# A row-sum kernel's last block: four loads of rows and two of columns regrouped into three and two

## The chip, the cores and the metric

The kernel runs on one core of one Trainium2 chip. The metric is the device time of that core in microseconds (us).

Two lengths appear. The *time* is what the timed runs give (163.94 us before). The *span* is what the profile covers of one execution (162.3 us).

## The reference

```python
def reference(x, multiplier):          # x: 32 x 512 x 1024 float32, multiplier 0.5
    return (np.sum(x, axis=-1) * multiplier).astype(np.float32)
```

There are 16,384 rows of 1024 numbers, 67.1 MB in all. Each row becomes one number.

## The kernel before

Each of the 128 partitions owns 128 consecutive rows. They are loaded in 8 blocks of 16 rows (8 MB each) into three rotating buffers. The first seven blocks are each one load. VectorE sums eight rows with one reduction, and ScalarE sums the other eight, one instruction a row, with the accumulator output.

The last block is loaded in pieces that get smaller, so that little work is left when the last bytes arrive. A row on VectorE is here a "half-add": one instruction adds the two halves of the row element by element and accumulates the total.

```python
    def dve_span(t, r, lo, hi, dst, start=0.0):      # VectorE, line 57
        mid = (lo + hi) // 2
        nc.vector.tensor_tensor_reduce(
            out=t[:, r, lo:mid], in0=t[:, r, lo:mid], in1=t[:, r, mid:hi],
            scale=mul, scalar=start, op0=ADD, op1=ADD, accum_out=dst)

    # ... seven blocks: one load, reduce_sum of 8 rows (line 73), act_row of 8 rows (line 47) ...

    c0 = (n_blocks - 1) * B
    t = x_pool.tile([P, B, D], fp32, name="xb")
    cut = 768
    pieces = [(0, 8), (8, 12), (12, 14), (14, 15)]
    for lo, hi in pieces:
        nc.sync.dma_start(out=t[:, lo:hi, :], in_=x_rows[:, c0 + lo : c0 + hi, :])
    for lo, hi in ((0, cut), (cut, D)):
        nc.sync.dma_start(out=t[:, B - 1, lo:hi], in_=x_rows[:, c0 + B - 1, lo:hi])
    on_act = {4, 5, 6, 7, 10, 11, 13}
    for r in range(B - 1):
        if r in on_act:
            act_row(t, r, c0 + r)
        else:
            dve_span(t, r, 0, D, res[:, c0 + r : c0 + r + 1])
    dve_span(t, B - 1, 0, cut, part)                                  # "first span"
    dve_span(t, B - 1, cut, D, res[:, rows - 1 : rows], start=part)   # "second span"

    nc.sync.dma_start(out=out_view, in_=res)                          # the store
```

## Time and profile before

| | before |
|---|---|
| time, median of 3 runs | 163.94 us (163.76 to 164.02) |
| span of the profiled execution | 162.3 us |
| share of the span: VectorE, ScalarE | 42%, 42% |
| read from memory | 67.11 MB, 414 GB/s over the span |

DVE is VectorE, ACT is ScalarE, SPq is the sync engine, which issues the transfers (DMA), and L57 is line 57 of the kernel. These are lines of the profile's page: the span, the engines' busy shares, what keeps each engine busy in 40 equal slices (a digit is the busy share in tenths), and the chain of waits that ended last, by line.

```profile
span 162.3 us, 234 instructions
DVE 68.2 (42%) x34; ACT 67.9 (42%) x127; POOL 0.2 (0%) x4
...
DVE  0000039800596007940099101990049700697452
ACT  3000039700595007930099101990039600696870
...
DMA  7979979979979979979989998998998997998990
...
DMA xb<-in_x_dram 85%; DVE sums L73 11%; SPq L90 1%; DVE xb L57 0%; SPq L71 0%; DVE part L57 0%; DVEq L135 0%
```

The DMA row is nearly full throughout (the packets took 96.5% of the span of the 16 DMA engines), while both compute engines pause in every block. The chain is 85% load. The 11% on VectorE are two reductions that release a buffer, after which the next load is queued long before its turn (the one issued at 51.09 landed 49.58 us later). So the kernel is a stream of loads, and everything ahead of the last block's own loads is out of reach of a change to that block.

The end of that chain, in order of time (start, length, what):

```profile
111.36 47.37 DMA xb<-in_x_dram
158.73 0.02 issue
158.75 0.35 DVE xb L57
159.11 0.13 issue
159.24 0.09 DVE part L57
159.33 0.03 issue
159.36 0.35 DVE xb L57
```

The timeline of the same end shows each instruction (start, length, engine, line, operation; in brackets the idle time before it and what ended it):

```profile
157.80 0.69 DVE L57 CUSTOM_DVE_ANT_0 xb<-xb 128x512 f32<-128x512 f32 x1 [0.58 <-DMA xb<-in_x_dram]
...
158.75 0.56 DVE L57 CUSTOM_DVE_ANT_0 xb<-xb 128x384 f32<-128x384 f32 x1 [0.26 <-DMA xb<-in_x_dram]
...
159.36 0.35 DVE L57 CUSTOM_DVE_ANT_0 xb<-xb,part 128x128 f32<-128x128 f32 x1
...
159.78 0.35 SPq L104 DMA_DIRECT2D out_dram<-res  x1
```

The first span starts when its 768 columns land, at 158.73. The second span has no bracket: its own 256 columns landed at 159.06, while VectorE was still on the first span. So the end hangs on the landing of the *first* part, then two half-adds in a row, then the store. Between the last landing (159.06) and the end of the span lie 3.2 us, 2% of the span. That is all the tail there is to save.

### The profile page before, as it was taken

What the parts mean: (1) busy time and instruction counts of PE and PEld (TensorE: products, weight loads), DVE (VectorE), ACT (ScalarE), POOL (GpSimd) and SP (SyncE); (2) the same over time, 40 slices, a digit from 0 to 9 for tenths busy, and PEclk for the clock granted to TensorE, in tenths of its full rate; (3) what the DMA queues carried; (4) which work ended last, traced back from release to release, by engine and by line L of the source; (5) the groups of instructions that cost most, each with busy time, mean ns of one, the idle gap of its engine ahead of it and who ended that gap; (6) DMA issues with size and microseconds to landing.
All of it is one profiled execution on the core that took longest, in us unless ns stands there. A gap on an engine that the chain in (4) does not pass through costs nothing.

```text
span 162.3 us, 234 instructions
## 1 busy us (share of the span) xinstructions
DVE 68.2 (42%) x34; ACT 67.9 (42%) x127; POOL 0.2 (0%) x4
## 2 busy tenths in 40 slices
DVE  0000039800596007940099101990049700697452
ACT  3000039700595007930099101990039600696870
POOL 0000000000000000000000000000000000000000
DMA  7979979979979979979989998998998997998990
GB/s 258 517 307 469 517 323 452 517 323 452 517 323 452 517 323 452 517 323 452 517 372 406 517 404 372 517 404 372 517 404 372 517 436 339 436 444 384 416 383 21
DMA packets 2017, 67.18 MB, mean 414 GB/s; under 512 B 224, under 2 KB 480, under 8 KB 736
## 3 DMA queue, kind: packets, MB, share of 16 engines
q1 hardware_dynamic: 2016, 67.18, 96.5%
q14 instruction: 1, 0.01, 0.0%
HBM read 67.11 MB, written 0.07 MB: 414 GB/s over the span
## 4 chain that ended last, share of the span: by engine, by line
DMA 85%; DVE 11%; SPq 1%; issue 0%; DVEq 0%
DMA xb<-in_x_dram 85%; DVE sums L73 11%; SPq L90 1%; DVE xb L57 0%; SPq L71 0%; DVE part L57 0%; DVEq L135 0%
## 5 line engine op out<-in xcount | busy, mean ns | idle before, releaser
L47 ACT ACTIVATE xb<-xb 128x1024 f32<-128x1024 f32 x63 | 65.6, 1042 | 89.1 <-DMA xb<-in_x_dram 89.1
L73 DVE TENSOR_REDUCE sums<-xb 128x8 f32<-128x8192 f32 x7 | 60.8, 8686 | 86.1 <-DMA xb<-in_x_dram 86.1
L47 ACT ACTIVATION_READ_ACCUMULATOR xb<-xb 128x1 f32 x63 | 11.7, 186 | 0.0
L57 DVE CUSTOM_DVE_ANT_0 xb<-xb 128x512 f32<-128x512 f32 (+1 forms) x9 | 5.8, 674 | 5.2 <-DMA xb<-in_x_dram 5.2
L47 ACT ACT_TABLE_LOAD x1 | 1.3, 1283 | 0.7 <-PEq L121 0.7
L76 DVE TENSOR_SCALAR res<-sums 128x8 f32<-128x8 f32 x7 | 1.2, 172 | 0.2
L57 DVE DVE_READ_ACCUMULATOR2_ANT res<- 128x1 f32 x9 | 0.7, 81 | 0.0
L57 DVE CUSTOM_DVE_ANT_0 xb<-xb,part 128x128 f32<-128x128 f32 x1 | 0.3, 350 | 0.0
L121 POOL MEMSET const-bfloat16-1.0<- 128x1 bf16 x1 | 0.1, 102 | 0.0
L121 POOL MEMSET const-uint8-127<- 128x1 uint8 x1 | 0.1, 102 | 0.0
L121 POOL MEMSET const-float32-1.0<- 128x1 f32 x1 | 0.1, 99 | 0.0
L121 POOL MEMSET const-float32-0.0<- 128x1 f32 x1 | 0.1, 98 | 0.2 <-issue 0.2
L57 DVE DVE_READ_ACCUMULATOR2_ANT part<- 128x1 f32 x1 | 0.1, 83 | 0.0
## 6 DMA issues: line engine op xcount, KB each, us to landing
xb<-in_x_dram SPq DMA_DIRECT2D x1, 4096.0 KB, 39.7
xb<-in_x_dram SPq DMA_DIRECT2D x1, 2048.0 KB, 44.2
xb<-in_x_dram SPq DMA_DIRECT2D x1, 1024.0 KB, 46.2
xb<-in_x_dram SPq DMA_DIRECT2D x1, 512.0 KB, 46.9
xb<-in_x_dram SPq DMA_DIRECT2D x1, 384.0 KB, 47.4
xb<-in_x_dram SPq DMA_DIRECT2D x1, 128.0 KB, 47.2
xb<-in_x_dram SPq DMA_DIRECT2D x7, 49.5
out_dram<-res SPq DMA_DIRECT2D x1, 64.0 KB, 1.5
```

What stands on the lines that cost most here:

```text
L47: nc.scalar.activation(out=t[:, r, :], in_=t[:, r, :], func=mybir.ActivationFunctionType.Copy, scale=mul, accum_out=res[:, col : col + 1],)
L57: nc.vector.tensor_tensor_reduce(out=t[:, r, lo:mid], in0=t[:, r, lo:mid], in1=t[:, r, mid:hi], scale=mul, scalar=start, op0=ADD, op1=ADD, ...
L73: nc.vector.reduce_sum(out=sums[:, c0 : c0 + h], in_=t[:, 0:h, :], axis=mybir.AxisListType.X)
L76: nc.vector.tensor_single_scalar(out=res[:, c0 : c0 + h], in_=sums[:, c0 : c0 + h], scalar=mul, op=mybir.AluOpType.mult,)
L90: nc.sync.dma_start(out=t[:, lo:hi, :], in_=x_rows[:, c0 + lo : c0 + hi, :])
L121: nc = _bacc.Bacc("TRN2", target_bir_lowering=False, num_devices=1)
```

## The change

The intent is to have one load fewer in the last block, and to give the last row's two parts sizes such that the second part lands about when VectorE is done with the first.

```diff
-    cut = 768
-    pieces = [(0, 8), (8, 12), (12, 14), (14, 15)]
+    cut = 640
+    pieces = [(0, 8), (8, 13), (13, 15)]
...
-    on_act = {4, 5, 6, 7, 10, 11, 13}
+    on_act = {4, 5, 6, 7, 11, 12, 14}
```

## The prediction

> **What bounds the kernel now.** It is a stream of loads. The chain of waits is 85% load and 11% one VectorE reduction (which only paces when a buffer comes free). 67.1 MB are read at 414 GB/s over the 162.3 us span; VectorE and ScalarE are each busy only 42%. The load engines show 97 to 99% busy up to the last block. Only the tail can react to this diff: the last block's loads are issued at 109.4 us, long before their turn, and everything before is untouched.
>
> **The tail now** (timeline, and the moments at which each load's completions arrive). The first 8 rows land at 149.11, then 4 rows at 154.00 (4.89 us), 2 rows at 156.49 (2.49), 1 row at 157.77 (1.28), 768 columns at 158.73 (0.96), 256 columns at 159.06 (0.33). VectorE starts the 768-column half-add at 158.75 (559 ns), reads its accumulator, and starts the 256-column one at 159.36 (350 ns), which therefore no longer waits for its own load: it waited for the previous span. It ends at 159.71; the store is issued at 159.78, and lands at 161.33. So the end is set by landing of the 768 columns + 0.61 + 0.35 us, then the store. [...]here the store took 1.55 us, and the change doesn't touch it.
>
> **What the change does.** The bytes are the same; one load fewer.
> 1. Loads. In the tail packets took 1213, 611, 309, 159, 124 and 46 ns for 32, 16, 8, 4, 3 and 1 KiB: about 0.038 ns/B plus about 8 ns. Each DMA engine moves 8 packets of a load, so one load fewer saves about 8 x 8 ns plus one 9 ns completion packet, 0.07 us. [...]Estimated landings: 8 rows 149.11, 5 rows 155.2, 2 rows 157.70, 640 columns 158.51, 384 columns 158.99.
> 2. Rows. Row pace is 0.615 us on VectorE and 1.04 us on ScalarE. Rows 8 to 10 and 11, 12 are done by 157.1 and 157.4, before the next load. Row 13 (VectorE) runs 157.72 to 158.4, free before the 640 columns land; row 14 (ScalarE) ends with its accumulator read at about 158.87. Neither is last.
> 3. The end. 640 columns: half-add about 0.49 us (559 minus 64 elements at 1 ns), so the second span starts at 158.53 + 0.54 = 159.07, just after its own load (158.99). It takes about 0.415 us (350 plus 64 elements), ending at 159.49 instead of 159.71. Store and end follow 0.22 us sooner.
>
> All of the gain, about 0.2 us, lies on the critical path, but it's 0.13% of the time; runs of before alone spread by 0.26 us. The whole stretch after the last landing is 3.2 us, 2% of the span, so a gain above 2% is not available, and a loss of 3.3 us would need a failure of the stream.
>
> **Predicted:** 163.73 us, range 163.40 to 164.00.
>
> **What would show it.** Right: last landing about 0.07 us sooner; the last two half-adds about 0.49 and 0.41 us, the second ending 0.2 us sooner; ScalarE's last row ending before it. Wrong: ScalarE's row 14 ends last, the larger 5-row load lands late enough to delay rows 11, 12 past 157.7, or 2560- and 1536-byte packets cost more than the line above says.
>
> **What would make it wrong.** Run-to-run drift larger than the effect; another rate on the next chip; the load start or a buffer's release shifting by chance.

## The result, and the profile after

| | before | after |
|---|---|---|
| time, median of 6 runs each | 163.97 us (163.76 to 164.09) | 163.84 us (163.62 to 164.17) |
| ratio, 95% interval | | 0.9994 (0.9981 to 1.0008) |
| span of the profiled execution | 162.3 us | 161.9 us |

A ratio here is the mean time of one kernel's runs over the mean of the other's in the same rounds, so it is not quite the ratio of the medians. The difference is far below 2%, and the interval includes 1.

The chain and the timeline of the changed kernel end so:

```profile
110.52 47.69 DMA xb<-in_x_dram
158.21 0.02 issue
158.23 0.49 DVE xb L57
158.72 0.02 DVE part L57
158.74 0.08 issue
158.82 0.42 DVE xb L57
```

```profile
157.41 1.06 ACT L47 ACTIVATE xb<-xb 128x1024 f32<-128x1024 f32 x1 [0.30 <-DMA xb<-in_x_dram]
...
158.23 0.49 DVE L57 CUSTOM_DVE_ANT_0 xb<-xb 128x320 f32<-128x320 f32 x1
158.37 0.19 ACT L47 ACTIVATION_READ_ACCUMULATOR xb<-xb 128x1 f32 x1
...
158.82 0.42 DVE L57 CUSTOM_DVE_ANT_0 xb<-xb,part 128x192 f32<-128x192 f32 x1
...
159.32 0.35 SPq L104 DMA_DIRECT2D out_dram<-res  x1
```

The two half-adds took 0.49 and 0.42 us, and ScalarE's last row ended at 158.56 (158.37 + 0.19), 0.26 us before the second of them started, all as predicted. The store is issued at 159.32 instead of 159.78.

Is that 0.46 us of gain? No. The right way to read a change in the tail of a stream is from a common point close ahead of it. The last full block is the same work in both kernels, and it landed at 139.40 us in one execution and at 139.08 us in the other. This splits the difference of the two profiled executions:

| stretch | before | after | difference |
|---|---|---|---|
| start of span to landing of last full block | 139.40 | 139.08 | -0.32 |
| that landing to issue of the store | 20.383 | 20.237 | -0.146 |
| issue of the store to its landing | 1.546 | 1.550 | 0.00 |
| landing of the store to end of span | 0.939 | 1.001 | +0.062 |

The first row is code that the change didn't touch. The last row was expected by nobody. These two rows, and whether 0.146 us can be believed at all, are what the experiments are about. "L" below stands for the landing of the last full block, and all stretches are counted from it.

### The profile page after: what moved, and what is told of

It reads as the page before. It is cut to its first block, busy times and chain, and to the rows that moved or that the text cites. A ratio compares the mean times of both kernels' runs of the same rounds, so it can differ in the third digit from the quotient of the medians.

```text
span 161.9 us, 233 instructions
## 1 busy us (share of the span) xinstructions
DVE 68.1 (42%) x34; ACT 67.9 (42%) x127; POOL 0.2 (0%) x4
## 4 chain that ended last, share of the span: by engine, by line
DMA 85%; DVE 11%; SPq 1%; issue 0%; DVEq 0%
DMA xb<-in_x_dram 85%; DVE sums L73 11%; SPq L90 1%; DVE xb L57 1%; SPq L71 0%; DVE part L57 0%; DVEq L135 0%
```

## The experiments

All twelve runs are here, in the order of their questions. The times of the kernel before beside them are from the same chip and the same rounds.

### What a measurement here can resolve

Edit: none, in two runs: the kernel before as it is, and the changed kernel as it is.

> The kernel before, unchanged, measured as if it were a change: the noise floor. Both theories: ratio 1.000 with an interval of about 0.1% to each side, so about 0.2 us, as wide as the effect that the change should have. In the profile, from the landing of the last full block to the issue of the store: 20.38 us within 0.03 us (20.383 in the first profile). If that stretch repeats so closely, it can measure the change where the total time cannot; if it moves by 0.1 us or more between executions of the same kernel, the 0.15 us seen in the first pair of profiles proves nothing.

> The changed kernel once more. Theory (the tail is shorter by 0.15 us, the rest of the difference between the first two profiles is drift of the stream): last full block to store issue 20.24 us within 0.03, total 0.1 to 0.2 us below the kernel before. Rival (the change also speeds the whole stream, which was 0.32 us ahead by the last full block in the first pair of profiles): last full block again lands 0.3 us sooner than in the profiles of before, and the total is 0.4 us lower.

Measured:

| run | median, us | before, us | ratio, 95% interval | L | L to store | landing to end |
|---|---|---|---|---|---|---|
| placebo | 163.89 | 163.91 | 0.9999 (0.9983 to 1.0016) | 139.19 | 20.387 | 0.939 |
| after_again | 163.76 | 163.91 | 0.9987 (0.9970 to 1.0003) | 139.28 | 20.215 | 1.001 |

The stretch from L to the store repeats to 0.004 us for the kernel before (20.383 and 20.387) and to 0.022 us for the changed one (20.237 and 20.215). So the 0.16 us between their means is real, although no interval of the total time could show it: those are about 0.3% (0.5 us) wide from end to end. L itself went from 139.08 to 139.28 for the changed kernel and from 139.40 to 139.19 for the kernel before, so the 0.32 us of the first pair was drift of the stream, and the rival that credited it to the change falls. The 0.062 us at the end of the span repeats exactly.

### Which half of the change gives what

```diff
 # cut_only: the kernel before, with
-    cut = 768
+    cut = 640
 # rows_only: the changed kernel, with
-    cut = 640
+    cut = 768
```

> The six loads and row shares of before, with only the cut of the last row moved from 768 to 640. Theory: landings after the last full block at 9.71, 14.61, 17.10, 18.38, 19.20, 19.68 us; second span starts at 19.81, store issue at 20.31 us, so 0.07 us of the 0.15. Rival (all the gain is one load fewer): 20.38, as before. Total time: same within noise under both.

> The new row pieces and row shares, with the old cut of 768. Theory: 9.71, 15.81, 18.31, 19.27, 19.60 us after the last full block, second span at 19.90, store issue at 20.32 us: 0.06 us of the 0.15 from one load fewer. Rival (the gain is all in the cut): 20.38. Total time: same within noise under both.

Measured:

| run | loads in last block | L to store | landing to end | L to end of span | ratio, 95% interval |
|---|---|---|---|---|---|
| before, placebo | 6 | 20.383, 20.387 | 0.939 | 22.868, 22.870 | |
| cut_only | 6 | 20.273 | 0.940 | 22.757 | 0.9996 (0.9981 to 1.0011) |
| rows_only | 5 | 20.315 | 1.001 | 22.869 | 1.0000 (0.9986 to 1.0015) |
| after, after_again | 5 | 20.237, 20.215 | 1.001 | 22.788, 22.771 | |

Both halves bring the store forward: the cut by 0.11 us (0.07 was expected; its last columns landed at 19.65 and not at 19.68), the load saved by 0.07 us, together about the 0.16 us of the whole change. But the 0.062 us at the end of the span comes with the load saved, and returns almost all of its 0.07 us. Counted to the end of the span, regrouping the rows gained nothing (22.869 against 22.868 and 22.870); the moved cut alone did all of it, and the full change is not better than cut_only.

### What a queued load costs, and how far merging may go

```diff
 # many_loads: the changed kernel, with
-    pieces = [(0, 8), (8, 13), (13, 15)]
+    pieces = [(r, r + 1) for r in range(B - 1)]
 # seven_rows: the changed kernel, with
-    pieces = [(0, 8), (8, 13), (13, 15)]
+    pieces = [(0, 8), (8, 15)]
```

> The changed kernel, but its first 15 rows of the last block in 15 loads of one row instead of 3: 12 loads more, each of 8 packets per DMA engine. Theory (a queued load costs only its packets' overhead, 8 x 8 ns plus a 9 ns completion): last landing and store issue 0.9 us later, store issue at 21.15 us after the last full block, total +0.9 us against the changed kernel. Rival 1 (bytes alone count): no change. Rival 2 (each load carries a fixed cost like the store's 1.5 us from issue to landing): +18 us.

> One step further in the direction of the change: rows 8 to 14 in one load of seven. Theory (merging rows is free only while the merged rows are computed before the last columns land): the seven rows land at 18.22 us after the last full block; VectorE then has 4 rows at 0.615 us before the last row's spans, so store issue at 21.76 us, 1.5 us later than in the changed kernel, although the last columns land 0.07 us sooner; total +1.5 us. Rival (fewer loads are always better in this stream): total 0.07 us lower.

Measured:

| run | median, us | before, us | ratio, 95% interval | L to last columns | L to store | landing to end |
|---|---|---|---|---|---|---|
| after_again (its times, from another chip, are above) | | | | 19.58 | 20.215 | 1.001 |
| many_loads | 164.56 | 164.08 | 1.0029 (1.0012 to 1.0046) | 20.45 | 21.074 | 0.853 |
| seven_rows | 165.53 | 164.08 | 1.0083 (1.0064 to 1.0103) | 19.50 | 21.728 | 1.059 |

With 12 more loads the store came 0.85 us later than in the changed kernel (21.074 less 20.226, the mean of its two profiles): 0.071 us a load. Neither rival fits. The end of the span shrank again, to 0.853 us, so that from L to the end it is 0.60 us more than before (23.471 against 22.869); the medians of the total differ by 0.48 us, the same within their noise. Against the changed kernel +0.9 us was expected in the total; the two were not timed in the same rounds, and from L to the end the difference is 0.69 us, because the end shrank.

In seven_rows the last columns land 0.08 us *sooner*, and the store comes 1.5 us *later*. Its timeline shows why (start, length, engine, operation):

```profile
157.71 0.69 DVE L57 CUSTOM_DVE_ANT_0 xb<-xb 128x512 f32<-128x512 f32 x1 [5.85 <-DMA xb<-in_x_dram]
...
159.55 0.69 DVE L57 CUSTOM_DVE_ANT_0 xb<-xb 128x512 f32<-128x512 f32 x1
...
160.16 0.49 DVE L57 CUSTOM_DVE_ANT_0 xb<-xb 128x320 f32<-128x320 f32 x1
...
160.69 0.42 DVE L57 CUSTOM_DVE_ANT_0 xb<-xb,part 128x192 f32<-128x192 f32 x1
```

VectorE idles 5.85 us for the seven rows, then has four of them back to back, and the last row's spans have to queue behind (no bracket at 160.16), although their columns had landed at 158.96. Merging rows was free here only as long as the merged rows were computed before the last columns arrived. The change's groups of five and two rows stay within that limit; one step further costs 1.5 us in the store's issue, against 0.16 us that the whole change gains there.

### Where the cut should be, and a wait that costs more than it should

```diff
 # cut512 and cut896: the changed kernel, with
-    cut = 640
+    cut = 512     # or 896
```

> The changed kernel with cut 512. Both theories: columns land at 18.97 and 19.61 us after the last full block, and the second span now truly waits for its own load. Theory (a wait for a load ends 0.02 us after it lands, as at the other loads): second span starts at 19.63, takes 0.48, store issue at 20.19 us, 0.05 sooner than the changed kernel. Rival (this instruction, which waits for its load and for the first span's sum, takes about 0.13 us from the later of the two, as the changed kernel's trace showed: landing 158.683, sum read by 158.73, start 158.817): start 19.75, store issue 20.31 us.

> The changed kernel with cut 896, away from the balance point on the other side. Theory: the first part lands at 19.43 us after the last full block, its half-add takes 0.62 us, second span starts at 20.12 and takes 0.28, store issue at 20.48 us: 0.24 us later than the changed kernel, though the last columns land at the same time. Rival (only the last landing sets the end): 20.24 or sooner, since the last span is shorter.

Measured from L, in us:

| run | first part lands | second part lands | second span starts | it takes | store |
|---|---|---|---|---|---|
| cut896 | 19.39 | 19.57 | 20.08 | 0.28 | 20.450 |
| after | 19.12 | 19.60 | 19.74 | 0.42 | 20.237 |
| cut512 | 18.98 | 19.59 | 19.73 | 0.48 | 20.297 |

Their total times tell nothing: cut896 164.20 us, ratio 1.0005 (0.9989 to 1.0022), and cut512 163.97 us, ratio 0.9996 (0.9977 to 1.0015), with 164.08 us for the kernel before.

Cut896 is as the theory said: a late and long first span pushes the second one, wherever the last landing is. For cut512 the theory falls and the rival holds. The second span now has the load as the last thing it waits for, and yet starts 0.13 us after the landing. In the records of all fourteen profiles, an instruction of VectorE or ScalarE whose only wait is for its load starts 0.02 to 0.03 us after the landing if it was idle until then. The chain of cut512 has two pieces there that such landings lack: a queue instruction (DVEq) and 0.09 us of "issue".

```profile
158.90 0.03 issue
158.92 0.02 DVEq L57
158.94 0.09 issue
159.03 0.48 DVE xb L57
```

The second span has two things to wait for: its load, and the first span's sum (`part`). The trace's own records show a separate semaphore instruction ahead of it on VectorE, which waits for the load (158.923 to 158.944); the half-add itself carries the wait for `part`. A semaphore is in these records a counter: in the kernel before, the landing of the last columns raises semaphore 105 until 159.060, and the separate instruction, from 159.088 to 159.109, waits for 105.

The same pattern stands in the kernel before, on the first half-add of the last block. It also has two waits: for its 8 rows, which landed at 149.106, and for ScalarE, which had been done for 40 us. The next piece's half-add waits for its load alone, which landed at 154.002:

```profile
149.25 0.69 DVE L57 CUSTOM_DVE_ANT_0 xb<-xb 128x512 f32<-128x512 f32 x1 [0.94 <-DMA xb<-in_x_dram]
...
154.03 0.69 DVE L57 CUSTOM_DVE_ANT_0 xb<-xb 128x512 f32<-128x512 f32 x1 [2.24 <-DMA xb<-in_x_dram]
```

The first starts 0.145 us after its landing, the second 0.024 us. The next run takes the second wait away by giving a wrong result in each partition's last row:

```diff
 # cut512_nosum: cut512, with
-    dve_span(t, B - 1, cut, D, res[:, rows - 1 : rows], start=part)
+    dve_span(t, B - 1, cut, D, res[:, rows - 1 : rows])
```

> The kernel of cut512, but its second span no longer takes the first span's sum as its start, so it waits for its load alone; the last row of each partition is wrong on purpose. Theory (an instruction with two waits gets the first one as an instruction of its own ahead of it, and the two together take 0.13 us after the landing): without the second wait the span starts 0.02 to 0.03 us after the landing at 19.59, so at 19.62 instead of 19.73 us after the last full block, and the store issue comes at 20.19 instead of 20.30. Rival (the delay belongs to the short last load or to an engine that was idle): still 19.73.

Measured: wrong as intended, one time of 163.80 us, state unknown, so only its profile counts. The columns land at 19.58 us after L, the second span starts at 19.61, the store is issued at 20.113.

```profile
158.94 0.02 issue
158.96 0.42 DVE xb L57
```

The wait is back to 0.02 us, so the theory of this run holds: the second wait is what costs the extra 0.11 us. The edit takes away two things at once, though, the wait and the start that is read from memory. That the start is not the cause is shown by the first half-add of the last block: its start is a constant, and it takes 0.144 us from landing to start even in this run, where it still has its two waits (0.138 to 0.145 us in the thirteen profiles in which the landing is its last wait). And a part nobody had predicted: the same half-add of 256 elements took 0.42 us instead of 0.48. Its start is now a constant and no longer a number for each partition read from memory.

### The end of the program

The runs so far had shown different times from the store's landing to the end of the span, and always the same for the same number of loads. The records of the sync engine explain it. When the program ends, that engine waits for the kernel's semaphores one after another in a fixed order. Here are the start times of these steps, relative to the store's landing, in us (the views of the profile leave semaphore instructions out; these are from the trace's records):

| step waits for semaphore | before (store signals 106) | after (store signals 105) | tiny3, below (store signals 108) |
|---|---|---|---|
| 104 | -1.146 | -1.150 | -1.144 |
| 105 and 103 | -1.088 | **0.016** | -1.085 |
| 106 and 100 | **0.016** | 0.078 | -1.024 |
| 107 and 99 | 0.081 | 0.142 | -0.960 |
| 108 and 102 | 0.142 | 0.204 | **0.016** |
| 101, then the closing barrier | 0.207 | 0.269 | 0.081 |
| end of span | 0.939 | 1.001 | 0.813 |

Steps ahead of the store's semaphore are done during the 1.1 us in which the store is under way. Those behind it come after, at 0.06 us each. The transfers take eight semaphores in turn (99, 100 and 103 to 108 in the records), so one load fewer moved the store from 106 to 105, one step earlier. Two earlier runs agree: the store of many_loads signalled 99, which the table has between 106 and 108 (0.853 us to the end, between 0.939 and 0.813), that of seven_rows 104, in the first step (1.059 us). If that is the cause, any extra transfer repairs it, even one that brings nothing:

```diff
 # tiny1 and tiny3: the changed kernel, with, in the loop over blocks after the load
+        if b == 2:
+            for k in range(1):        # tiny3: range(3)
+                scrap = res_pool.tile([P, 1], fp32, name=f"scrap{k}")
+                nc.sync.dma_start(out=scrap[0:1, :], in_=x_rows[0:1, 0, k : k + 1])
```

> The changed kernel plus one load of 4 bytes, issued while the queue waits for a buffer, its result unused. Theory (at the end of the program the sync engine waits for the kernel's load semaphores one after another in a fixed order, 0.06 us a step, and only the steps behind the store's own semaphore come after its landing; one load fewer moved the store to a semaphore one step earlier): the store is on the same semaphore as before again, and from its landing to the end of the span 0.94 us instead of 1.00; all else as in the changed kernel (store issue 20.22 us after the last full block). Rival (the 1.00 us has to do with the shape of the last loads): 1.00 still.

> The same with three such loads, so that the store takes the last semaphore of that order. Theory: 0.82 us from the store's landing to the end of the span, store issue 20.22 us after the last full block, so 0.19 us less than the changed kernel and about 0.29 us (0.18%) less than before: the fastest of all, total about 163.6 us, though the interval may still touch 1. Rival: 1.00 us, and the three loads cost their own time, 0.02 us or more.

> The kernel of tiny3 once more, because its first interval (0.9971 to 0.9995) ends close to 1. Theory: ratio again about 0.998, and 20.20 us from the last full block to the store issue, 0.81 us from the store's landing to the end of the span, as in the first run. Rival (the first ratio was luck): ratio 1.000, although the stretches in the profile are the same.

Measured:

| run | median, us | before, us | ratio, 95% interval | L to store | landing to end | L to end of span |
|---|---|---|---|---|---|---|
| tiny1 | 163.97 | 164.00 | 0.9994 (0.9982 to 1.0006) | 20.210 | 0.939 | 22.698 |
| tiny3 | 163.77 | 164.00 | 0.9983 (0.9971 to 0.9995) | 20.198 | 0.813 | 22.554 |
| tiny3_again | 163.82 | 164.01 | 0.9992 (0.9979 to 1.0006) | 20.198 | 0.813 | 22.560 |

The end of the span did in each case what the order of the semaphores says: 0.939 with the store on 106 again, 0.813 on 108. Tiny3 has the shortest tail of all correct kernels, 0.31 us less than before and 0.22 us less than the change. In the total time one of its two intervals lies just below 1 and the other includes it. So its tail is shown to be shorter than both kernels'; its total time is faster than before in one run of two, by less than 0.2%, and its lead over the changed kernel's total was not compared in the same rounds. Three useless loads for 0.19 us are a demonstration, not a recommendation.

## Why the prediction was right

The range held (163.84 us in 163.40 to 164.00), and so did the statement that a gain above 2% was not available. Neither is evidence for the mechanism: the median of the unchanged kernel, 163.97 us, lies in that range too. Point by point:

1. *A stream of loads bounds it, only the tail can react.* Right. L moved by up to 0.4 us between executions (139.08 to 139.50 over these runs) without regard to the tail's code.
2. *Loads: about 0.038 ns a byte plus 8 ns a packet, one load fewer saves 0.07 us.* Right (the packets listed there give 0.037 ns a byte). Predicted landings of the two column parts, counted from L = 139.40: 19.11 and 19.59; measured 19.12 and 19.60. Many_loads gave 0.071 us a load. The 8 ns a packet are an estimate from the trace before: a straight line through 1 KiB at 46 ns and 32 KiB at 1213 ns leaves about 8 ns at no bytes. In the changed kernel's trace 1.5 KiB took 65 ns and 2.5 KiB 102 ns, on the same line.
3. *Rows 8 to 14 are off the critical path.* Right: ScalarE's row 14 ended at 19.48 after L, the second span began at 19.74. Seven_rows showed where this ends.
4. *The second span starts 0.54 us after the first, 0.2 us sooner in all.* This step was mis-sized. It started 0.59 us after the first (19.74 against 19.15), because with the new cut it is the wait for its own load that holds it longest, and with the semaphore instruction ahead of it that wait ends not 0.02 but 0.13 us after the landing. In the records the separate instruction that waits for the load ended at 159.109 in the kernel before, hidden behind the first span (which ended at 159.314), and at 158.731 in the changed kernel, 0.01 us after the first span's end; from there to the half-add it took another 0.086 us. That this is the same cost as in cut512 is shown by the traces: from landing to start the second span takes 0.133 to 0.135 us in all eight profiles in which that wait holds it longest (after, after_again, cut_only, many_loads, cut512 and the three with tiny loads), whether the landing came 0.07 us before the first span's end or 0.17 us behind it. The prediction had the load land only 0.08 us ahead of the start and counted no such wait, although the kernel before showed one at its first half-add (149.106 to 149.25). The second span's length, 0.415 predicted at 1 ns an element (the trace before had 559 ns for 384 elements and 691 for 512), was 0.419. The store came 0.15 and 0.17 us sooner (the two profiles), not 0.22.
5. *Store and end follow.* The store took 1.55 us in both, as said. "End" was wrong by 0.062 us: the fewer load moved the store's semaphore forward in the closing order. Of the 0.22 us, then, about 0.06 were lost ahead of the store, most of it at the second span's start, another 0.06 after the store, and 0.08 to 0.10 us arrived (22.788 and 22.771 against 22.868 and 22.870).
6. *The cost of a transfer.* The store showed 1.55 us from issue to landing (1.546 before, 1.550 after). Many_loads shows that such a cost is not paid by each of the loads that stand in a queue: there a load more cost 0.071 us.

The total moved by 0.13 us in the medians, and by -0.10 and -0.23 us in the means of the two comparisons (after and after_again). That agrees with the 0.09 us of the tail, and with 0.22, and with nearly nothing. The total alone could not have told a right mechanism from a wrong one.

## What to carry to other kernels

When a change is worth less than the runs' own spread, measure it from the nearest event ahead of it that both versions share, check with an unchanged kernel how well that stretch repeats, and only then believe or doubt it. At the end of this stream, the best of the cuts was the one whose last bytes landed just as the engine got free (at 640 the store came at 20.237 and 20.215 us; with the same rows it came at 20.297 for 512, 20.315 for 768 and 20.450 for 896), and a step further with the merging of loads cost far more than the load saved: 1.5 us against 0.07. Count the waits of the last instruction too: a second one cost 0.11 us here (a correct kernel without it was not tried). And look at what comes after the last useful instruction: removing a transfer can shift the order in which the program closes (0.062 us here).

## What the traces add

- An instruction with two waits: in the records a semaphore instruction stands ahead of it and takes one of them. When the wait for a load held them longest, VectorE started 0.13 to 0.15 us after the landing with a semaphore instruction ahead, ScalarE 0.10 to 0.11 us, and both 0.02 to 0.03 us without.
- The length of a half-add: with a constant as its start, 491 ns for 320 elements (after) and 559 for 384 (before). With a number for each partition read from memory as its start, 419 ns for 192 elements (after) and 350 for 128 (before). A straight line through the first two would give 355 and 287 ns for 192 and 128 elements, an estimate, so about 0.06 us for such a start; the same 256 elements took 0.48 us with it (cut512) and 0.42 us without (cut512_nosum).
- The closing waits of these programs come in an order in which the semaphore of the last transfer has its place: 0.06 us a step, 0.813 to 1.059 us from the store's landing to the end of the span, and each run with a transfer more or less moved it (seven_rows 1.059, after 1.001, tiny1 0.939, many_loads 0.853, tiny3 0.813).
- Two costs of the sync engine's queue: a further load in a full queue cost 0.071 us, and the lone store at the end took 1.55 us to land.
